# Sums of feed-forward weights formed in scratch by accumulating DMAs, and preparation steps placed after every pair

## Chip, cores, metric

The kernel runs on one core of one Trainium2 chip. The metric is the device time of one execution in microseconds (us); lower is better.

## What is computed

One step of a two-layer decoder trunk over 536 token columns (528 prompt positions and 8 samples), all in float32:

```
x += 0.5 * FFN1(rms(x));  x += MIX(rms(x));  x += 0.5 * FFN2(rms(x))     in each of 2 layers
swiglu(h) = (silu(h @ W_gate) * (h @ W_up)) @ W_down       1024 -> 2 x 2816 -> 1024
MIX of layer 0: convolution module and sliding-window attention; MIX of layer 1: a complex-diagonal state-space model (SSM)
a last RMSNorm follows
```

There are thus four feed-forwards, called FF1 (layer 0, first), FF2 (layer 0, second), FF3 (layer 1, first) and FF4 (layer 1, second) here. The output also holds the convolution, key, value and SSM states.

## The kernel before, in words

**Layout.** The activations stand transposed: `x[0..7]` are eight tiles of 128 model rows by 536 token columns, in two halves of 268. `xh` and `xl` are x times the norm's gain, split into a part that TensorE takes exactly and the rest; `eh`, `el`, `fh`, `fl` hold sums and differences of them. A product of a weight tile (`whi`, `wlo`: 128 x 128) with such a pair takes three matmuls of 268 columns: hi by hi, hi by lo, lo by hi.

**One feed-forward** is `ffn` (L401). The 2816 hidden columns are 22 tiles of 128, in three chunks of 6, 8 and 8 (`CHUNKS`, L33). The first two hidden tiles (three in FF1) are made by `pair` (L383): the gate gemm, then `rstd` (L304), which makes the normaliser `R` out of one matmul, a ScalarE operation and eight VectorE operations (`rsqrt`, L290), then the up gemm, then the evacuation by VectorE with R (L395 to L398) and the split `put` (L145). Between the pairs, `operands(k)` (L187) makes the sums and differences for four k, seven VectorE operations each (with `put`), and `settle` (L206) moves a part of them.

All other hidden tiles, 20 per feed-forward and 19 in FF1, are made by `seven` (L246), called a *pair* (gate and up) here. It forms the four quarter products of the two halves of the tokens with seven products instead of eight (a scheme of Strassen's kind): 7 x 4 x 3 = 84 matmuls (L266). `SLOTS` (L32) gives the order, in which a pair's last two products run among the next pair's first. `seven_weights` (L212) loads gate and up weights G and U (two DMAs of 512 KB, L220, L221), splits G, and forms on VectorE

```
q = U0 + U1        (L228)      0, 1: the upper and lower half of the 1024 model rows
U0 = U0 + G0       (L229)
G0 = G0 + q        (L230)      G1 = G1 + G0 (L234)
```

and splits all of them: the high part by ScalarE (L224), the low part by VectorE (L225). G and U take turns in four `raw` buffers; the split weights of one pair fill the three `whi` and three `wlo` buffers. After a chunk, its down projection runs over eight tiles of model rows (called column tiles here): a gemm (L139, L142) of the chunk's hidden tiles, and an addition to x on VectorE (L434); after the last chunk also `finalize` (L151).

**Preparation.** `setup0` (L440) prepares the layer 0 mixer beside FF1, and `ssm_prep` (L909) the SSM beside FF2 and FF3: parameters by series of small VectorE operations, powers `pw` (L981), powers E of the transition (L999 to L1027, complex products through `cmul`, L895), and for each of eight j the tables B, C, K and T (L1029 to L1086), written to scratch by POOL's DMA queue and read back by the mixer. Both are Python generators: `fill` (L405) draws steps from them, and only the down loops call it (L437): one step per column tile in the first chunk, two in the second, one for the first four of the last, 28 per feed-forward.

**Order of work.** Each engine runs its instructions in one fixed order, which the framework's list scheduler derives when the kernel is built, out of program order and a timeline of its own; an operation that this timeline takes to be ready may be put well ahead of its place in the program. Weight DMAs are issued from SP's queue, preparation's from POOL's (some from ScalarE's).

## Time and profile before

| | |
|---|---|
| median of 3 runs | 2019.54 us (2015.43 to 2019.72) |
| the profiled execution | 2020.43 us |
| its span, first to last instruction | 2018.6 us |
| TensorE busy (PE) | 1933.7 us, 96% |
| VectorE busy (DVE) | 1577.0 us, 78% |
| ScalarE busy (ACT) | 938.1 us, 46% |
| GpSimd busy (POOL) | 81.4 us, 4% |
| mean granted TensorE clock | 0.984 of full |

The engines run beside each other, so shares don't add up. A row of busy time by stretch gives the stretch in us from the span's start, its length, the busy us and in brackets the count of instructions for PE (matmuls), PEld (weight loads), DVE, ACT and POOL, the granted clock of TensorE as a share of full speed, the busy share of the 16 DMA engines, and GB/s. Overlapping instructions of one engine count once in a stretch; the mean in ns of a group by line is that of one instruction with its overlap. A wait row gives the engine and operation that waited, what ended the wait, the sum in us, how often and the longest. In a timeline the brackets at the end give the idle time before the operation and what ended it.

FF1 runs from about 55 to 422 us, FF2 from 656 to 1048, FF3 from 1048 to 1433, FF4 from 1635 to the end.

### The profile page before, as it was taken

What the parts mean: (1) busy time and instruction counts of PE and PEld (TensorE: products, weight loads), DVE (VectorE), ACT (ScalarE), POOL (GpSimd) and SP (SyncE); (2) the same over time, 40 slices, a digit from 0 to 9 for tenths busy, and PEclk for the clock granted to TensorE, in tenths of its full rate; (3) what the DMA queues carried; (4) which work ended last, traced back from release to release, by engine and by line L of the source; (5) the groups of instructions that cost most, each with busy time, mean ns of one, the idle gap of its engine ahead of it and who ended that gap; (6) DMA issues with size and microseconds to landing.
All of it is one profiled execution on the core that took longest, in us unless ns stands there. A gap on an engine that the chain in (4) does not pass through costs nothing.

```text
span 2018.6 us, 37789 instructions
## 1 busy us (share of the span) xinstructions
PE 1933.7 (96%) x15338; PEld 1870.4 (93%) x15338; DVE 1577.0 (78%) x2799; ACT 938.1 (46%) x1639; POOL 81.4 (4%) x160
## 2 busy tenths in 40 slices
PE   6999999999999899999999999999989999999998
PEld 5999999998779899898999999999989999999997
DVE  5768769678868999989789997696694486794876
ACT  5535435434446635435465354354324364452543
POOL 2000000000000000020001210000110000000000
PEclk9899999999989999999999999999999999999999
DMA  6233333321005234353334543236583323333231
GB/s 185 81 107 87 95 95 95 116 75 44 27 22 123 65 94 127 121 156 113 102 94 120 163 130 103 86 102 193 164 261 101 90 63 95 95 111 89 84 105 53
DMA packets 372066, 213.51 MB, mean 106 GB/s; under 512 B 36299, under 2 KB 362503, under 8 KB 371869
## 3 DMA queue, kind: packets, MB, share of 16 engines
q1 hardware_dynamic: 354901, 190.63, 32.8%
q0 software_dynamic: 6432, 19.40, 3.0%
q10 hardware_dynamic: 10560, 1.09, 0.4%
q8 instruction: 120, 1.97, 0.4%
q14 instruction: 53, 0.43, 0.1%
HBM read 193.14 MB, written 23.65 MB: 107 GB/s over the span
## 4 chain that ended last, share of the span: by engine, by line
PE 73%; DVE 14%; DMA 5%; issue 4%; ACT 3%; ACTq 0%; POOL 0%; SPq 0%; DVEq 0%; POOLq 0%
PE mm L266 25%; PE mm L139 18%; PE mm L142 9%; PE S L139 7%; PE S L266 4%; PE S L142 4%; DMA raw<-in_ffn_w_gu 3%; DVE wlo L225 2%; PE S L747 1%; ACT whi L128 1%; DVE ml L149 1%; DVE wlo L129 1%; DVE ql L225 1%; DMA pb<-in_x_prompt 1%; DVE raw L229 1%
## 5 line engine op out<-in xcount | busy, mean ns | idle before, releaser
L224 ACT ACTIVATE whi<-raw 128x1024 fp32r<-128x1024 f32 (+1 forms) x237 | 216.9, 916 | 184.1 <-PE mm L266 50.5
L128 ACT ACTIVATE whi<-raw 128x1024 fp32r<-128x1024 f32 (+2 forms) x166 | 159.6, 973 | 303.3 <-PE mm L139 156.7
L139 PE MATMUL mm<-mh,whi 128*128 128x268 f32 x1224 | 262.1, 291 | 5.9 <-ACT whi L128 3.0
L225 DVE TENSOR_TENSOR wlo<-raw,whi 128x1024 fp32r<-128x1024 f32 (+1 forms) x237 | 246.7, 1041 | 25.5 <-ACT whi L224 24.7
L139 PE MATMUL mm<-ml,whi 128*128 128x268 f32 x1224 | 259.5, 287 | 0.1
L142 PE MATMUL mm<-mh,wlo 128*128 128x268 f32 x1224 | 259.5, 288 | 0.1
L129 DVE TENSOR_TENSOR wlo<-raw,whi 128x1024 fp32r<-128x1024 f32 (+2 forms) x166 | 184.5, 1117 | 70.1 <-ACT whi L128 67.7
L139 PEld LDWEIGHTS mm<-mh,whi 128*128 128x128 f32 x1224 | 194.5, 190 | 10.6 <-ACT whi L128 4.1
L142 PEld LDWEIGHTS mm<-mh,wlo 128*128 128x128 f32 x1224 | 194.5, 189 | 1.6 <-DVE wlo L129 1.2
L139 PEld LDWEIGHTS mm<-ml,whi 128*128 128x128 f32 x1224 | 194.9, 189 | 0.7 <-DVE ml L149 0.4
L266 PE MATMUL mm<-xh,whi 128*128 128x268 f32 x632 | 183.6, 291 | 5.9 <-ACT sn L274 5.3
L266 PE MATMUL mm<-eh,wlo 128*128 128x268 f32 x632 | 181.5, 287 | 3.2 <-DVE wlo L225 3.2
L266 PE MATMUL mm<-eh,whi 128*128 128x268 f32 x632 | 182.4, 289 | 1.8 <-ACT whi L224 1.1
L266 PE MATMUL mm<-xh,wlo 128*128 128x268 f32 x632 | 181.0, 286 | 0.0
L266 PE MATMUL mm<-xl,whi 128*128 128x268 f32 x632 | 180.8, 286 | 0.0
L266 PE MATMUL mm<-el,whi 128*128 128x268 f32 x632 | 180.6, 286 | 0.0
L266 PEld LDWEIGHTS mm<-xh,whi 128*128 128x128 f32 x632 | 119.0, 188 | 10.6 <-ACT sn L274 9.6
L139 PE MATMUL S<-mh,whi 128*128 128x268 f32 x568 | 121.3, 289 | 3.0 <-ACT mh L148 1.6
L266 PEld LDWEIGHTS mm<-eh,wlo 128*128 128x128 f32 x632 | 118.8, 188 | 4.2 <-DVE wlo L225 4.0
L266 PEld LDWEIGHTS mm<-eh,whi 128*128 128x128 f32 x632 | 119.1, 188 | 3.6 <-ACT whi L224 1.6
L142 PE MATMUL S<-mh,wlo 128*128 128x268 f32 x568 | 120.1, 287 | 0.3 <-DVE wlo L129 0.3
L266 PEld LDWEIGHTS mm<-xl,whi 128*128 128x128 f32 x632 | 119.1, 189 | 0.0
(520 smaller groups left out, 5079.7 us busy)
## 6 DMA issues: line engine op xcount, KB each, us to landing
raw<-in_ffn_w_gu SPq DMA_DIRECT2D x174, 512.0 KB
raw<-in_ffn_w_down SPq DMA_DIRECT2D x64, 512.0 KB
raw<-in_ffn_w_down SPq DMA_DIRECT2D x32, 384.0 KB
raw<-in_ssm_w_glu SPq DMA_DIRECT2D x16, 512.0 KB
raw<-in_ab_w_in SPq DMA_DIRECT2D x10, 512.0 KB
dB<-B POOLq DMA_DIRECT2D x16, 256.0 KB, 2.9
dC<-Z POOLq DMA_DIRECT2D x32, 128.0 KB, 3.2
dT<-dK POOLq DMA_DIRECT2D x8, 512.0 KB, 5.0
```

Of the source, the lines that this page charges most:

```text
L128: nc.scalar.activation(hi[:, :K], raw[:, :K], AF.Copy)
L129: nc.vector.tensor_sub(lo[:, :K], raw[:, :K], hi[:, :K].bitcast(F32))
L139: nc.tensor.matmul(ps[:, h, :HT], hi[:, k, :], src[:, h * HT:(h + 1) * HT], start=(k == 0 and i == 0), stop=False)
L142: nc.tensor.matmul(ps[:, h, :HT], lo[:, k, :], xh[k][:, h * HT:(h + 1) * HT], start=False, stop=(k == K - 1))
L149: nc.vector.tensor_sub(lo, src, hi.bitcast(F32))
L224: nc.scalar.activation(h, r, AF.Copy)
L225: nc.vector.tensor_sub(l, r, h.bitcast(F32))
L229: nc.vector.tensor_add(U[:, k0], U[:, k0], G[:, k0])
L266: nc.tensor.matmul(ps, w[:, c + k, :], b[k], start=bool(first and k + i == 0), stop=bool(last and k == 3 and i == 2), skip_group_check=True)
L747: nc.tensor.matmul(S[:, g, :w], qT[t][rw, 128 * b:128 * b + 128], kT[rw, k0:k0 + w], start=False, stop=True)
```

## The change

For FF2, FF3 and FF4 the first two sums (L228, L229) are no longer made by VectorE. One feed-forward ahead (FF2's during FF1, FF3's during FF2, FF4's during FF3), `presum` forms them in DRAM scratch for all 2816 columns: for each of the two arrays of 512 x 2816, eight slices of 64 rows are copied DRAM to DRAM and the other summand is then added by an accumulating DMA, all from POOL's queue, 32 steps in all. The accumulating DMA of a slice is issued after the copy of the next. `seven_weights` then loads q (into one of two buffers now) and U0 from scratch and only U1 from the weights: four DMAs, 1.25 MB, instead of two with 1 MB.

`fill` is now called after each pair as well as after each column tile, for one step of the preparation each time (44 times per feed-forward, 43 in FF1). With `behind`, the step's instructions on an engine are queued behind given ones: after a pair, VectorE's behind the split of its result; after a column tile, VectorE's behind the addition to x, TensorE's behind the gemm and ScalarE's behind the weights' split. In FF1 to FF3 each call also has POOL copy one column of the tile just made (`go`) and queues a step of `presum` behind that copy. `ssm_prep` gets more yields, so its work is cut into 61 steps instead of 52, and two operations on the C table become one. At a feed-forward's start all four `operands` follow the first `pair`, their VectorE work behind R, and the weight work of the first two pairs of `seven` on VectorE is queued behind the end of the first `pair`. The DMA descriptor scratch is cut to 8192 bytes.

```diff
+    def behind(self, *ins):
+        with ExitStack() as scope:
+            for i in ins:
+                scope.enter_context(self.tc.issue_after(i.ins))
+            yield
...
+    def presum(self, wgu, n):
+        out = [self.dr.tile([512, D_FF], F32, name=f"{a}{n}") for a in ("dP", "dQ")]
+        A = lambda i, j: wgu[512 * j:512 * j + 512, D_FF * i:D_FF * i + D_FF]
+        def steps():
+            late = None
+            for o, a, b in ((out[0], A(1, 0), A(1, 1)), (out[1], A(0, 0), A(1, 0))):
+                for r in range(0, 512, 64):
+                    r = slice(r, r + 64)
+                    nc.gpsimd.dma_start(o[r], a[r])
+                    yield
+                    if late:
+                        nc.gpsimd.dma_start(*late[:2], accum_op=OP.add, max_dma_last_dim=5632)
+                        yield
+                    late = o[r], b[r]
+            nc.gpsimd.dma_start(*late, accum_op=OP.add, max_dma_last_dim=5632)
+            yield
...
-    def seven_weights(self, gu, f):
+    def seven_weights(self, gu, f, sums):
-        q = self.fx.tile([128, 4, 128], F32, name="q4")
+        q = self.fx.tile([128, 4, 128], F32, name="q4", bufs=2)
         nc.sync.dma_start(G[:], gu[:, :, f:f + 128])
-        nc.sync.dma_start(U[:], gu[:, :, D_FF + f:D_FF + f + 128])
+        if sums:
+            part = lambda t: t[:].rearrange("(k p) f -> p k f", p=128)[:, :, f:f + 128]
+            nc.sync.dma_start(q[:], part(sums[0]))
+            nc.sync.dma_start(U[:, k0], part(sums[1]))
+            nc.sync.dma_start(U[:, k1], gu[:, k1, D_FF + f:D_FF + f + 128])
+        else:
+            nc.sync.dma_start(U[:], gu[:, :, D_FF + f:D_FF + f + 128])
...
-        nc.vector.tensor_add(q[:], U[:, k0], U[:, k1])
-        nc.vector.tensor_add(U[:, k0], U[:, k0], G[:, k0])
+        if not sums:
+            nc.vector.tensor_add(q[:], U[:, k0], U[:, k1])
+            nc.vector.tensor_add(U[:, k0], U[:, k0], G[:, k0])
...
-                w = self.seven_weights(gu, (f0 + n0 + n) * 128)
+                with self.behind(*([first] if first and n < 2 else [])):
+                    w = self.seven_weights(gu, (f0 + n0 + n) * 128, sums)
...
-                self.put(self.mh[n0 + n][:], self.ml[n0 + n][:], b[:])
+                fill(1, self.ml[n0 + n], self.put(self.mh[n0 + n][:], self.ml[n0 + n][:], b[:]))
...
-        def fill(n):
-            for _ in range(n):
-                next(filler, None)
+        def fill(n, t, *ins):
+            if n:
+                with self.behind(*ins):
+                    next(filler, None)
+            if pre:
+                i = nc.gpsimd.tensor_copy(self.go[:], t[:, :1].bitcast(F32))
+                with self.behind(i):
+                    next(pre, None)
...
-                for f in range(n0):
-                    self.pair(gu, f, head if f == 0 else None)
-                    for k in range(4 * f // n0, 4 * (f + 1) // n0):
+                first = self.pair(gu, 0, head)
+                for k in range(4):
+                    with self.behind(self.on_r):
                         self.operands(k)
+                for f in range(1, n0):
+                    self.pair(gu, f, None)
...
-                fill((1 if nf < 8 else 2) if not last else int(d < 4))
+                fill(1, self.x[d], i, self.on_pe, self.on_act)
...
-                nc.vector.tensor_add(w[0][:, :576], w[0][:, :576], w[1][:, :576])
-                nc.vector.tensor_scalar(CL[:, :, 1], v(w[0]), -1.0, None, op0=OP.mult)
+                nc.vector.tensor_sub(CL[:, :, 1], v(w[1]), v(w[0]))
...
-    nc = bacc.Bacc("TRN2", target_bir_lowering=False, num_devices=1)
+    nc = bacc.Bacc("TRN2", target_bir_lowering=False, num_devices=1, dynamic_dma_scratch_size=8192)
```

`on_r` is the last VectorE operation of R, `on_pe` the last matmul of the latest gemm, `on_act` the ScalarE split of the latest weight tile.

## Rows read from the trace of the kernel before

**Rows 1.** The page, busy time of TensorE, its share of the span and instructions.
```profile
PE 1933.7 (96%) x15338; PEld 1870.4 (93%) x15338; DVE 1577.0 (78%) x2799; ACT 938.1 (46%) x1639; POOL 81.4 (4%) x160
```

**Rows 2.** Busy time by stretch: FF2, FF3, FF4 but its last columns, FF1.
```profile
656.00:1048.00 392.00, 375.55 (x2975) 366.20 (x2975) 350.51 (x754) 188.99 (x315) 20.08 (x38) 0.99 0.38 111
1048.00:1433.00 385.00, 377.72 (x3046) 369.49 (x3045) 313.32 (x488) 185.72 (x307) 28.32 (x53) 1.00 0.42 125
1635.00:1950.00 315.00, 308.49 (x2450) 304.18 (x2449) 245.95 (x374) 156.18 (x259) 0.00 (x0) 1.00 0.32 93
55.00:422.00 367.00, 362.50 (x2865) 358.00 (x2866) 267.47 (x400) 169.45 (x275) 2.43 (x8) 0.99 0.33 94
```

**Rows 3.** Busy time by stretch: pairs of two chunks of FF2, of FF4; FF2's start.
```profile
756.00:843.00 87.00, 82.93 (x653) 80.96 (x652) 85.49 (x194) 48.17 (x80) 1.63 (x3) 1.00 0.37 111
...
901.00:989.00 88.00, 84.05 (x673) 81.80 (x672) 83.96 (x136) 48.68 (x84) 6.93 (x13) 1.00 0.39 116
...
1732.00:1815.00 83.00, 81.59 (x651) 80.58 (x650) 73.19 (x112) 47.96 (x81) 0.00 (x0) 1.00 0.34 99
...
660.00:664.00 4.00, 2.89 (x24) 2.48 (x23) 4.00 (x11) 2.44 (x6) 0.00 (x0) 1.00 0.00 0
664.00:668.00 4.00, 0.60 (x4) 0.33 (x3) 4.00 (x14) 3.27 (x6) 0.00 (x0) 0.69 0.00 0
668.00:672.00 4.00, 3.99 (x18) 4.00 (x19) 4.00 (x11) 3.28 (x8) 0.00 (x0) 0.50 0.04 12
```

**Rows 4.** Waits of TensorE's weight loads in FF2: us in total, times, longest.
```profile
PEld S L139 <- DVE ta L395: 3.6, 1, 3.6
PEld mm L266 <- DVE wlo L225: 3.5, 3, 1.3
```

**Rows 5.** Groups of instructions by line, whole span.
```profile
L228 DVE TENSOR_TENSOR q<-raw 128x512 f32<-128x512 f32 x79 | 54.4, 689 | 45.1 <-DMA raw<-in_ffn_w_gu 44.7
```

**Rows 6.** Timeline of VectorE at the start of FF2: start, us, operation.
```profile
657.90 0.81 DVE L299 TENSOR_TENSOR tb<-ta 128x268 f32<-128x268 f32 x2 [0.74 <-ACT ta L297]
...
667.25 0.71 DVE L395 TENSOR_TENSOR ta<-S,R 128x536 f32<-128x536 f32 x1
667.87 0.70 DVE L397 TENSOR_TENSOR tb<-mm,R 128x536 f32<-128x536 f32 x1
```

**Rows 7.** Groups by line, VectorE, 656 to 1200 us.
```profile
L1061 DVE TENSOR_TENSOR w<-w,w 128x576 f32<-128x576 f32 x8 | 6.0, 750 | 0.0
...
L887 DVE TENSOR_TENSOR we<-E 128x16 f32<-128x16 f32 (+4 forms) x12 | 3.8, 317 | 0.0
...
L887 DVE TENSOR_TENSOR pt<-E 128x16 f32<-128x16 f32 x12 | 2.2, 182 | 0.0
```

**Rows 8.** Waits of TensorE's weight loads in FF4 without its end.
```profile
PEld mm L139 <- ACT eh L148: 2.5, 1, 2.5
```

**Rows 9.** DMA queues (packets, MB, share of 16 engines) and issues (us to landing).
```profile
q0 software_dynamic: 6432, 19.40, 3.0%
...
dT<-dK POOLq DMA_DIRECT2D x8, 512.0 KB, 5.0
```

**Rows 10.** Timelines of SP's queue and of VectorE beside a pair of FF4.
```profile
1749.95 0.37 SPq L221 DMA_DIRECT2D raw<-in_ffn_w_gu  x1
...
1753.96 0.69 DVE L228 TENSOR_TENSOR q<-raw 128x512 f32<-128x512 f32 x1 [1.24 <-DMA raw<-in_ffn_w_gu]
...
1755.51 1.22 DVE L225 TENSOR_TENSOR wlo<-raw,whi 128x1024 fp32r<-128x1024 f32 x1
...
1758.53 0.69 DVE L230 TENSOR_TENSOR raw<-raw,q 128x512 f32<-128x512 f32 x1
```

**Rows 11.** Timelines of POOL and of VectorE in the SSM mixer.
```profile
1442.43 0.19 POOL L1144 COPY us<-us 128x8 f32<-128x8 f32 x1 [6.36 <-DVE us L1143]
...
1464.61 1.12 POOL L1144 COPY us<-us 128x8 f32<-128x8 f32 x1 [1.51 <-DVE us L1143]
...
1464.46 1.21 DVE L129 TENSOR_TENSOR wlo<-raw,whi 128x1024 fp32r<-128x1024 f32 x1
```

More of the change, by code (lines that the diff above doesn't have):

```diff
@@ L1 @@
-from contextlib import ExitStack
+from contextlib import ExitStack, contextmanager
 import numpy as np
@@ L89, in open @@
         self.R = t("R", F32)
+        self.go = self.cst.tile([128, 1], F32, name="go")
         self.sq = t("sq", F32)
@@ L141, in gemm @@
             for h in hs:
-                nc.tensor.matmul(ps[:, h, :HT], lo[:, k, :], xh[k][:, h * HT:(h + 1) * HT],
-                                 start=False, stop=(k == K - 1))
+                self.on_pe = nc.tensor.matmul(ps[:, h, :HT], lo[:, k, :], xh[k][:, h * HT:(h + 1) * HT],
+                                              start=False, stop=(k == K - 1))
     def put(self, hi, lo, src):
@@ L244, in seven_weights, with seven @@
                 "P7": (uh, ul, 0, X(self.eh, r), X(self.el, r))}
-    def seven(self, gu, f0, n0, nf):
+    def seven(self, gu, f0, n0, nf, first, sums, fill):
         nc = self.nc
@@ L310, in rstd @@
             nc.tensor.matmul(ps[h], self.ones[:], self.sq[:, hc[h]], start=True, stop=True)
-        self.rsqrt([self.R[:, c] for c in hc], ps)
+        self.on_r = self.rsqrt([self.R[:, c] for c in hc], ps)
     def load(self, gu):
@@ L416, in ffn @@
                 n0 = 3 if head else 2
-                for f in range(n0):
-                    self.pair(gu, f, head if f == 0 else None)
-                    for k in range(4 * f // n0, 4 * (f + 1) // n0):
+                first = self.pair(gu, 0, head)
+                for k in range(4):
+                    with self.behind(self.on_r):
                         self.operands(k)
+                for f in range(1, n0):
+                    self.pair(gu, f, None)
                 self.settle()
-            self.seven(gu, f0, n0, nf)
+            self.seven(gu, f0, n0, nf, first if f0 == 0 else None, sums, fill)
             dn = wdn[f0 * 128:(f0 + nf) * 128].rearrange("(k p) f -> p k f", p=128)
@@ L981, in ssm_prep @@
         for k in range(8):
+            if k % 2 == 0:
+                yield
             self.cmul(pw[:, 0, :, k + 1], pw[:, 1, :, k + 1], pw[:, 0, :, k], pw[:, 1, :, k],
@@ L1011, in ssm_prep @@
                         bc = lambda a: a[:, :, m:m + 1].to_broadcast([128, 16, n - 1])
-                        self.cmul(e[0][:, :, m + 1:m + n], e[1][:, :, m + 1:m + n], e[0][:, :, 1:n], e[1][:, :, 1:n],
-                                  bc(e[0]), bc(e[1]), w1, w2)
+                        steps = self.cmul_steps(e[0][:, :, m + 1:m + n], e[1][:, :, m + 1:m + n], e[0][:, :, 1:n], e[1][:, :, 1:n],
+                                                bc(e[0]), bc(e[1]), w1, w2)
+                        for _ in steps:
+                            if n > 16:
+                                yield
                         if n > 4:
@@ L1394, in run @@
             prep = self.ssm_prep(p)
-            self.ffn(io["ffn2_w_gu"][0], io["ffn2_w_down"][0], 3, prep)
-            self.ffn(io["ffn1_w_gu"][1], io["ffn1_w_down"][1], 4, prep)
+            more, pre = self.presum(io["ffn1_w_gu"][1], 1)
+            self.ffn(io["ffn2_w_gu"][0], io["ffn2_w_down"][0], 3, prep, sums, pre)
+            self.finish(pre)
+            sums, pre = self.presum(io["ffn2_w_gu"][1], 2)
+            self.ffn(io["ffn1_w_gu"][1], io["ffn1_w_down"][1], 4, prep, more, pre)
             self.finish(prep)
+            self.finish(pre)
         self.mixer1(5)
-        self.ffn(io["ffn2_w_gu"][1], io["ffn2_w_down"][1], None, fin=True)
+        self.ffn(io["ffn2_w_gu"][1], io["ffn2_w_down"][1], None, sums=sums, fin=True)
 def constants():
```

27 lines of the change are left out of this document (18 added, 9 removed).

## The prediction

> **What bounds the kernel now.** I read the page first, then the busy time by feed-forward and by stage, then the waits of the weight loads of TensorE, and last the timelines of VectorE and the queues at the places where TensorE stood still. The page shows TensorE busy for 1933.7 of 2018.6 us [rows 1]. The change takes no matmul away, so time can be won only from the 85 us in which TensorE idles. FF1 to FF4 are the four feed-forwards in the order in which they run. TensorE idles for 392 - 375.55 = 16.5 us in FF2, 385 - 377.72 = 7.3 in FF3, 315 - 308.49 = 6.5 in the part of FF4 shown and 367 - 362.50 = 4.5 in FF1 [rows 2]. FF1 has the same loops and almost no preparation beside them; its 4.5 us are my floor for what stays. A matmul takes 308.49 / 2450 = 0.126 us [rows 2].
>
> Why FF2 is worse: VectorE is busy for 85.5 of 87 us and 84.0 of 88 us beside the eight pairs of its second and third chunk, and for 73.2 of 83 us beside the same eight pairs in FF4, where nothing is prepared [rows 3]. So the preparation of the SSM fills VectorE, and TensorE waits for weight splits and for evacuations by VectorE: 3.5 us and 3.6 us are the longest two rows of FF2's waits [rows 4].
>
> **The change, part by part.**
>
> *The two additions.* Each pair of FF2 to FF4 loses the adds of L228 and L229, 0.689 us busy for the one [rows 5] and, being of the same shape, as much for the other. Neighbours on VectorE start a little before the one ahead has ended (two of 0.71 us start 0.62 apart [rows 6]), so I count 0.60 each: 1.2 us for each of 20 pairs, 24 us per feed-forward. Only the part that lies where VectorE is the bound counts. A pair takes TensorE 83 / 8 = 10.4 us; VectorE needs 73.2 / 8 = 9.15 us of it now and 7.95 after, which leaves 2.4 us beside a pair for a preparation step.
>
> *The preparation steps* were pulled 28 times per feed-forward, all in the down loops (two per column tile in the second chunk), and are now pulled once after each of 20 pairs and 24 column tiles, 44 times. There are 61 of them instead of 52, so 44 run in FF2 and 17 in FF3. I count which step falls where from the yields. The first chunk takes the small ones. The eight pairs of the second chunk take eight of the ten steps of the powers E. These cost six lines like L887's 12 x 0.317 and six like its 12 x 0.182 us [rows 7], 6 x 3.8 + 6 x 2.2 = 36 us with overlaps, some 27 without, 20 of it on those eight pairs: 2.5 to 3 us per pair. With 7.95 that is 10.5 to 11, no less than TensorE's 10.4. I expect nothing from these pairs; their 87 - 82.9 = 4.1 us idle stays. The third chunk's steps belong to the tiles j: five steps for six operations of the size of L228, six of the size of L1061 (0.75 us [rows 7]) and some small ones; a scaling besides is dropped. That is 6 x 0.69 + 6 x 0.75 + 0.6 = 9.2 us, under 1.8 per step with the overlaps taken off, 9.7 with the pair, below 10.4. Of the 88 - 84.05 = 3.95 us idle there [rows 3] I take 2.5, since FF4's pairs keep 83 - 81.59 = 1.4. From FF2's other stretches, the down loops above all, I take 1.5.
>
> *The start of a feed-forward.* In FF2 the normaliser R begins at 657.90, and the first evacuation that needs it starts at 667.25 [rows 6], because operand and weight work is mixed in between the eight operations of R. TensorE idles for 1.1 and 3.4 us from 660 to 668, and its granted clock is 0.69 of full, then 0.50 (the lower level, 1.2 GHz): 18 matmuls in 4 us where 0.126 us each would give 32, 1.8 us more [rows 3]. In all 6.3 us. The change puts the operands behind R, the first two pairs' weight work behind pair 0, and the preparation later; eight operations of some 0.4 us [rows 6] then end near 661.5 and TensorE hardly stops. It gives some back: about two of four operand groups, seven operations each (six of 268 columns, of which two took 0.81 us [rows 6], and one of 536 at 0.62: 3 us), ran ahead of R and now follow it, 6 us later for the sixth product of the first pair, against 2.4 us of adds gone. I take +4 in FF2, between 0 and 6.3. In FF3 and FF4 the same order is a gain of at most the 2.5 us that FF4 waits there [rows 8] and a loss of at most 3 each; I take 0 and +1. From the rest of FF3 (7.3 less the floor of 4.5, half of it) I take 1.5.
>
> *The sums in scratch.* Each of FF1, FF2, FF3 gets 16 copies and 16 accumulating transfers of 64 x 2816 x 4 B = 0.72 MB, paced by one step per pair or column tile. The POOL queue's packets took 3.0% of 16 engines for 19.40 MB, 3.1 us per MB [rows 9]: a copy is 2.25 us of all engines. No accumulating transfer is in the trace. Its ends are 2.25 us (a copy) and 21 us (three passes, each at the 5.0 us that dT's DRAM-to-DRAM 0.52 MB needs to land [rows 9], scaled up to 7 us). I take 4.5, twice a copy, because it reads twice as much and the queue's own rate is the nearest row. What it can hurt are weight loads. In FF4 the up half was issued at 1749.95, VectorE's add waited for it until 1753.96, and the result is first needed at 1758.53 [rows 10]: 3.9 us to spare after the add's 0.69. In FF1, which still adds, 2.25 us is covered by that and 4.5 is not quite; I take a loss of 1.5 us (0 to 15). In FF2 to FF4 the first sum is loaded by itself into one of two buffers, ahead of the up half, and two sums are no longer in the chain, so the cover grows; the 256 KB more per pair and two more issues (0.37 us each on SP's queue [rows 10]) I cost at nothing behind it.
>
> *POOL.* After each pair and column tile of FF1 to FF3 POOL copies one column to pace itself, 43 + 44 + 44 = 131 copies, with the transfers and the preparation's own queued behind them. POOL is busy for 20 and 28 us of FF2 and FF3 [rows 2], so it has the time. A copy of 128x8 took 0.19 us at 1442.43 and 1.12 us at 1464.61, where it ended together with a VectorE operation of 1.21 us that had begun before it [rows 11]; elsewhere an operation of that shape takes 1.22 us [rows 10]. So POOL waits and VectorE does not: nothing. The Trainium skill, SBUF — State Buffer, section "Who interferes with whom", says that whichever of the two starts first holds their shared port for its whole instruction, so the copy could as well hold VectorE up. By that rule the sum would lose up to 1.12 us per copy; the rows show the other order.
>
> *The sum.* FF2 2.5 + 1.5 + 4 = 8; FF3 1.5; FF4 1; FF1 -1.5: 9 us. The profiled execution took 2020.43 us, 1.8 more than its span and 0.9 more than the median, 2019.54. 2020.4 - 9 = 2011.4, and less 0.9 that is **2010.5 us**.
>
> **The rivals.**
> *VectorE stays the bound (0.22).* The relief of 24 us in FF2 is eaten: as much preparation is now pulled in FF2 (44 of 61 steps against 28 of 52), the E steps fall on pairs, and the operands behind R delay three starts. For it: 10.5 to 11 against 10.4 us; against it: the third chunk has room. It keeps 2.5 + 1.5 of the gains and loses 1.5: 2017.
> *The accumulating transfers hold up the weights; slower (0.18).* If one occupies the engines for 9 us, each of the eight that lie beside pairs of FF1 delays a load by up to 9 - 3.9 = 5.1 us, half of them or half of that seen by TensorE: 8 x 2.6 = 20 us against 9 won, 2030. It decides from about 5.2 us per transfer, where 8 x 1.3 eats the gain. For it: DMA engines are already busy 38 and 42% of FF2 and FF3 [rows 2]. Against it: they are far from full.
> *POOL's copies hold VectorE (0.04).* 44 x 1.12 = 49 us more in FF2 would leave VectorE at 350.5 - 24 + 49 of 392, the bound again, and about 12 us worse in all: 2032. This is the skill's rule with the other order of starts.
> My forecast has 0.56.
>
> **How the numbers follow.** A measurement of this kernel can tell about 0.2%, 4 us, from no change. The forecast's case is faster nearly throughout (0.54 of 0.56). The second splits 0.08 faster, 0.12 same, 0.02 slower. The third and fourth are slower but for 0.01. Together 0.62 faster, 0.15 same, 0.23 slower. The range starts where all idle time above the floor goes (FF2 12 + 1.8, FF3 2.8, FF4 2.5, about 19 us, 2000, less 1) and reaches to the third case, 2030; the forecast's own range is 2001 to 2016.
>
> **What would show it.** Right: L228 and L229 only 19 times; the idle of TensorE in FF2 down to about 8 us; R's first evacuation within 5 us of R's start and no fall of the clock there; FF1 within 2 us of its 367. Wrong: in FF1 longer waits of VectorE for weight loads than before, with TensorE waiting for splits; or VectorE full beside FF2's second-chunk pairs with TensorE as idle as before; or a new stall at the sixth product at the start of FF3 and FF4.

## The result and the profile after

The changed kernel took **2073.15 us** (median of 4 runs, 2070.96 to 2076.23), the kernel before beside it 2019.63: a ratio of **1.027 (1.0246 to 1.0291)**, 54 us slower. The forecast was 2010.5, in a range of 1999 to 2030. Both the sign and the range were wrong.

The profile page of the changed kernel, its rows of busy time, of two DMA queues (packets, MB, share of 16 engines) and of the transfers (KB each, median us from issue to landing), to be read against [rows 1, 9]:

```profile
PE 1955.0 (94%) x15338; PEld 1888.9 (91%) x15338; DVE 1506.4 (73%) x2671; ACT 934.5 (45%) x1639; POOL 248.1 (12%) x387
...
q1 hardware_dynamic: 387541, 206.37, 34.4%
q0 software_dynamic: 17184, 88.61, 16.8%
...
dP<-in_ffn_w_gu POOLq DMA_DIRECT2D x48, 704.0 KB, 7.0
dQ<-in_ffn_w_gu POOLq DMA_DIRECT2D x48, 704.0 KB, 6.8
```

VectorE lost 1577.0 - 1506.4 = 70.6 us of work, as the change meant. The time got longer all the same. Busy time by stretch, FF1, FF2, FF3 and FF4 of the changed kernel (columns as in [rows 2]):

```profile
core 0: us, PE busy (x) PEld busy (x) DVE busy (x) ACT busy (x) POOL busy (x), PEclk, DMA share, GB/s
53.00:449.00 396.00, 370.20 (x2846) 360.54 (x2845) 269.34 (x417) 172.02 (x283) 53.73 (x85) 0.98 0.54 146
677.00:1092.00 415.00, 386.35 (x3027) 376.58 (x3027) 338.90 (x741) 189.04 (x319) 89.08 (x127) 0.98 0.65 178
1092.00:1488.00 396.00, 378.22 (x3009) 371.15 (x3008) 288.41 (x442) 186.79 (x309) 75.36 (x116) 0.98 0.68 186
1689.00:2004.00 315.00, 309.70 (x2456) 306.69 (x2455) 228.99 (x349) 157.47 (x266) 0.00 (x0) 0.99 0.37 107
```

TensorE now idles for 25.8 us in FF1 (4.5 before), 28.7 in FF2 (16.5) and 17.8 in FF3 (7.3) [rows 2]. These three are the feed-forwards with transfers beside them. FF4, without any, idles for 5.3 (6.5; a part of what its start loses is busy time at a lower clock, below). FF1 is the plainest: it uses no sums, has next to no preparation, and is 29 us longer. Its groups by line show where that comes from. First the addition of the kernel before in the window of FF1, then the same one after:

```profile
L228 DVE TENSOR_TENSOR q<-raw 128x512 f32<-128x512 f32 x18 | 12.4, 690 | 10.1 <-DMA raw<-in_ffn_w_gu 9.9
```

```profile
L267 DVE TENSOR_TENSOR q<-raw 128x512 f32<-128x512 f32 x19 | 13.1, 689 | 39.5 <-DMA raw<-in_ffn_w_gu 39.5
```

VectorE stood still for 39.5 us ahead of this addition, waiting for a weight load; before it was 9.9. TensorE meets that a little later, as waits for evacuations and splits. The waits of TensorE's weight loads in FF1, two of the kernel before and then the four longest of the changed kernel (us in total, times, longest; L314 and L317 of the changed kernel are L274 and L277 of the one before, and no wait of `seven` for a split, L224 or L225, is among its rows):

```profile
PEld mm L266 <- ACT sn L274: 2.7, 6, 0.7
...
PEld mm L266 <- DVE tb L277: 0.4, 1, 0.4
```

```profile
PEld mm L306 <- ACT sn L314: 7.5, 7, 1.7
PEld mm L306 <- DVE tb L317: 6.3, 7, 1.2
PEld mm L306 <- ACT whi L262: 6.1, 3, 3.5
PEld mm L306 <- DVE wlo L263: 5.0, 2, 4.6
```

### The profile page after: what moved, and what is told of

Its sections match the earlier page's. It is cut to its first block, busy times and chain, and to the rows that moved or that the text cites. A ratio compares the mean times of both kernels' runs of the same rounds, so it can differ in the third digit from the quotient of the medians.

```text
span 2073.8 us, 38318 instructions
## 1 busy us (share of the span) xinstructions
PE 1955.0 (94%) x15338; PEld 1888.9 (91%) x15338; DVE 1506.4 (73%) x2671; ACT 934.5 (45%) x1639; POOL 248.1 (12%) x387
## 3 DMA queue, kind: packets, MB, share of 16 engines
q0 software_dynamic: 17184, 88.61, 16.8%
## 4 chain that ended last, share of the span: by engine, by line
PE 72%; DVE 9%; DMA 8%; ACT 3%; issue 2%; ACTq 0%; SPq 0%; DVEq 0%; POOLq 0%
PE mm L306 29%; PE mm L148 15%; PE mm L151 8%; PE S L148 6%; DMA raw<-in_ffn_w_gu 5%; PE S L306 5%; PE S L151 3%; DVE wlo L263 2%; DMA raw<-in_ffn_w_down 1%; PE S L796 1%; ACT whi L262 1%; DMA dE<-E 1%; ACT whi L129 1%; DVE ml L158 1%; DVE wlo L130 1%
## 5 line engine op out<-in xcount | busy, mean ns | idle before, releaser
L306 PE MATMUL mm<-xh,whi 128*128 128x268 f32 x632 | 186.7, 296 | 20.6 <-ACT whi L262 8.4
L306 PE MATMUL mm<-xh,wlo 128*128 128x268 f32 x632 | 185.8, 294 | 3.5 <-DVE wlo L263 3.5
L306 PEld LDWEIGHTS mm<-eh,whi 128*128 128x128 f32 x632 | 121.7, 193 | 17.8 <-ACT sn L310 15.9
L306 PEld LDWEIGHTS mm<-xh,wlo 128*128 128x128 f32 x632 | 122.5, 194 | 4.4 <-DVE wlo L263 4.2
## 6 DMA issues: line engine op xcount, KB each, us to landing
raw<-in_ffn_w_down SPq DMA_DIRECT2D x32, 384.0 KB
```

What stands on the lines that cost most here:

```text
L306: nc.tensor.matmul(ps, w[:, c + k, :], b[k], start=bool(first and k + i == 0), stop=bool(last and k == 3 and i == 2), skip_group_check=True)
```

## The experiments

Ratios are to the kernel before on the same chip, with a 95% interval. "Stage" times are differences between the ends of VectorE's evacuations in the traces of one execution each; the time of a feed-forward runs from the first VectorE operation of its R to the addition of its last column tile (FF4: to the end). One thing about the code first: in `seven` the parameter `first` is overwritten by the start flag of the first product, so the changed kernel holds only the first pair's weights behind pair 0, not those of two.

### Which part costs: transfers and start undone

The theory to begin with was that the transfers starve the weight loads, above all beside column tiles; the rival, that the new start and the order of the steps cost.

**Transfers out.** `presum` issues nothing, and the loads of the sums read plain weights. POOL's pacing copies stay.

```
-        return out, steps()
+        return [A(1, 0), A(0, 0)], iter(())
```

> The changed kernel without any transfer into scratch: the loads that read sums read weights of the same shape instead, so q and U0 hold plain weights and the output of the feed-forwards is not the reference's; POOL's pacing copies stay. Theory 1 (the transfers' packets of 5.6 and 11.3 KB starve the weight queue's packets of 512 B, above all in the down loops): the 8 to 9 us that each first-chunk down loop of FF1 to FF3 has lost come back, FF1 is as long as before, and the whole is about 45 us faster than the changed kernel, 2025 to 2032. Theory 2 (the new order of the start and of the preparation is what costs): at most 10 us faster than the changed kernel, 2063 or more.

**Old start.** The operands spread between the first pairs as before, nothing held behind R or pair 0.

```
-                for k in range(4):
-                    with self.behind(self.on_r):
-                        self.operands(k)
+                    for k in range(4 * f // n0, 4 * (f + 1) // n0):
+                        self.operands(k)
```

> The changed kernel with the operands spread between the first pairs as before and nothing queued behind R or pair 0. Theory 1: the start costs little beside the transfers; from R to the last pair of the first chunk FF2, FF3 and FF4 had become 2, 3.5 and 6.5 us longer, so at most 12 us come back, 2061 to 2067. Theory 2: 30 us or more come back, below 2045.

**Both.**

> Both undone: no transfer (weights read in place of the sums, so again not the reference's output), and the operands at a start as before. What is left is the gain that the change was to bring: two adds less per pair and the preparation beside every pair. Theory 1 and my forecast of that part: 8 to 13 us faster than before, 2007 to 2013. Theory 2 (preparation beside pairs fills VectorE): no faster than before, 2018 to 2035.

**Transfers alone.** The kernel before with the 96 transfers and the pacing copies beside it, their results unused.

```
+                pace(self.ml[n0 + n])       # beside every pair
+                pace(self.x[d])             # beside every column tile
```

> The kernel before with the 96 transfers, POOL's pacing copies and the smaller descriptor scratch of the change beside it, at the same places; the results are read by nobody, all adds and the old order stay. Theory 1: FF1, FF2 and FF3 grow by some 15 us each, 2060 to 2075, and nothing else changes. Theory 2: within 8 us of before, below 2028.

| | new start | old start |
|---|---|---|
| with transfers | 2073.15, 1.0268 (1.0246 to 1.0291) | 2052.54, 1.017 (1.0149 to 1.0191) |
| without | 2031.32, 1.0057 (1.004 to 1.0075) | 2011.89, 0.997 (0.9953 to 0.9987) |

The transfers cost 41.8 us with the new start and 40.6 with the old one; the new start costs 20.6 and 19.4. The two hardly touch each other. The run without transfers came out as the theory said; the old start alone fell between the two cases, since both causes are there. What is left with both undone gains 0.3%. In the kernel before, whose VectorE has more to do, the transfers alone made it 2109.85 us, 1.0453 (1.0417 to 1.0489): twice their cost in the changed kernel, and more than either case expected.

### Where the transfers cost

With the transfers and without (old start in both), FF1 takes 396.7 for 374.2 us, FF2 389.8 for 374.7 and FF3 381.1 for 375.5. Stage times put the largest part into the column tiles after the first chunk, where the loop of eight should take 30 us:

| stage | without | with |
|---|---|---|
| first chunk's column tiles, FF1 / FF2 / FF3 | 30.5 / 31.9 / 30.4 | 37.8 / 39.1 / 39.3 |
| FF1: second chunk from first to last pair, its column tiles | 77.4, 36.8 | 82.6, 40.4 |
| FF1: third chunk's first pair, the other seven | 20.5, 77.6 | 25.5, 81.9 |
| second chunk's first pair, FF1 / FF2 / FF3 | 23.1 / 20.1 / 27.2 | 20.0 / 21.1 / 23.1 |
| FF2: second chunk from first to last pair, its column tiles, third chunk's first pair | 76.2, 39.3, 22.3 | 77.3, 43.2, 24.8 |
| FF3: second and third chunk's pairs | 74.1, 75.1 | 74.1, 75.1 |

That is 23.4 us in the first row, of which the pair behind gives 6 back, 18 in the rest of FF1, 7 beside the second chunk of FF2, and nothing beside the later pairs of FF3. POOL's timeline at this place in FF1 of the changed kernel:

```profile
118.34 1.06 POOL L236 DMA_DIRECT2D dP<-in_ffn_w_gu  x1 [0.36 <-issue]
...
122.22 0.55 POOL L233 DMA_DIRECT2D dP<-in_ffn_w_gu  x1 [0.28 <-issue]
...
123.09 0.97 POOL L236 DMA_DIRECT2D dP<-in_ffn_w_gu  x1
...
124.79 0.53 POOL L233 DMA_DIRECT2D dP<-in_ffn_w_gu  x1
...
129.03 0.96 POOL L236 DMA_DIRECT2D dP<-in_ffn_w_gu  x1
...
133.13 0.53 POOL L233 DMA_DIRECT2D dP<-in_ffn_w_gu  x1 [0.26 <-issue]
```

Six transfers in 15 us. One takes 3.0 us of all 16 engines: the queue's share rose from 3.0% [rows 9] of 2018.6 us to 16.8% of 2073.8, 288 us more for 96. The packet records of the changed kernel's trace tell the two kinds apart: 3,072 packets of 11,264 bytes make 2.0 us for a copy, 6,144 of 5,632 bytes 4.0 us for an accumulate. Six are 18 us of engine time in 15, beside the weight loads. The chain of waits shows the load that suffered, with its addition behind it:

```profile
125.70 18.09 DMA raw<-in_ffn_w_gu
143.79 0.02 issue
143.82 0.70 DVE q L267
```

A load that took about 4 us beside a pair of FF4 [rows 10] held the chain for 18.1; its issue alone held SP's queue for 11.2 us, where that of [rows 10] took 0.37. **None in the first chunk** tests that: old start, big packets, no transfer beside the first chunk, what is left over two at a time in the third. (Not to a column tile alone, as the expectation has it: `ins` is not empty behind pairs either, and the trace has two transfers behind each pair of FF1's third chunk.)

```
-            if pre:
+            if pre and f0:
                 ...
+                    if last and ins:
+                        next(pre, None)
```

> The changed kernel with the old start (2052.5 us), its 96 transfers in their big packets, but none beside a feed-forward's first chunk; the ones left over go two to a column tile in the third chunk. The first chunk's down loops took 37.8, 39.1 and 39.3 us with transfers and 30.5, 31.9 and 30.4 without, 23 of the 41 us that the transfers cost. If it is the burst of transfers in that stage that costs (they are more than the engines can move in the time): about 2030, up to 2038 us with what the third chunk's pairs of transfers cost. If a transfer costs the same wherever it stands: 2048 to 2056 us.

2034.51 us, 1.0063 (1.0048 to 1.0078): 18 of the 41 us are gone. The first chunk's column tiles are back at 30.7, 31.8 and 30.7 us. That agrees with the 23.4 less 6 of the table. So it is shown that the transfers issued in this stage cost what is lost there. FF1 gains next to nothing in all (394.8 for 396.7 us), since the doubled transfers take it back in its third chunk (87.3 us for 77.6 without transfers).

### Packets or bytes

In the changed kernel the transfers' packets are 11,264 and 5,632 bytes, those of a weight load 512. The Trainium skill (DMA: Bandwidth & Descriptors, "Queues, rings and completion order") says that an engine alternates between its queues and drains a whole packet of one before it turns to the next; a packet there holds several descriptors, so it need not be what the profile counts as one. The trace agrees as far as the queues' shares go: by the packet records the weight queue had 0.10 to 0.15 of the engines from 128 to 137 us of the changed kernel, while big packets ran beside it, and 0.33 to 0.50 from 129 to 150 us of the first run below, with small ones. My theory 1a was that a load beside a queue of big packets gets few bytes, and that equal packets would give it half of the engine.

```
-                    nc.gpsimd.dma_start(o[r], a[r])
+                    nc.gpsimd.dma_start(o[r], a[r], max_dma_last_dim=512)      # and 5632 -> 512 for both accumulates
```

> The changed kernel with the same 96 transfers cut into packets of 512 bytes, the size of a weight load's, in place of 11,264 (copies) and 5,632 (accumulates). Theory 1a (what starves the weight loads is the size of the packets: an engine that serves its queues packet by packet spends 490 ns on a transfer's and 28 ns on a weight load's, so the load keeps a few per cent of the engine): with equal packets the loads keep half of the engine, most of the 41 us that the transfers cost comes back, 2031 to 2050 us. Theory 1b (the engines' time for the bytes is what lacks, whatever the packets): 2065 to 2080 us. If the small packets make the accumulates dearer, each a read and a write of its own, it is slower than the changed kernel, over 2080 us.

> The small packets, and the operands of a feed-forward spread between its first pairs as in the kernel before, nothing held behind the norm or the first pair. The start gave 19 to 21 us in both settings measured, so this is the small-packet run less 20 us: theory 1a 2011 to 2030 us, theory 1b 2045 to 2060 us.

> The run without transfers in the first chunk (2034.5 us, big packets), with the small packets. Without transfers at all it is 2011.9. What is left of their cost stands beside the first feed-forward's second and third chunk: 3.5 us in the second chunk's pairs, 4.2 in its down loop, 5.5 and 9.7 in the third chunk's pairs. If there the packets starve the weight loads and not the bytes: 2016 to 2024 us. If the bytes: 2031 to 2038 us.

2066.69 us, 1.023 (1.0212 to 1.0249), with the new start; 2040.9, 1.0111 (1.0087 to 1.0135), with the old one; and without the first chunk's transfers 2050.74, 1.0149 (1.0127 to 1.0171), **16 us slower** than with big packets. The first fits the rival (bytes), the second lies between the two cases, the third is slower than both. Rows of the page of the first of them, to be held against those of the changed kernel above:

```profile
q0 software_dynamic: 84000, 88.61, 21.2%
...
dP<-in_ffn_w_gu POOLq DMA_DIRECT2D x48, 704.0 KB, 9.6
```

The packet counts say that the accumulates came out at 512 bytes and the copies at 4,096 (48 x 1408 + 48 x 176 packets are the 84,000 less the 7,968 that both kernels have besides). The same bytes now take (0.212 x 2069.3 - 60.6) / 96 = 3.9 us of all engines for 3.0; by the packet records a copy still takes 2.0 us, an accumulate 5.9 for 4.0. The stages, with the old start, show that the small packets free the loads in some places and cost time in others:

| stage | none | big | small |
|---|---|---|---|
| first chunk's column tiles, FF1 / FF2 / FF3 | 30.5 / 31.9 / 30.4 | 37.8 / 39.1 / 39.3 | 37.6 / 32.9 / 34.6 |
| FF1: second chunk's pairs, third chunk's first pair, the other seven | 77.4, 20.5, 77.6 | 82.6, 25.5, 81.9 | 77.0, 21.5, 78.0 |
| FF2: second chunk's pairs, its column tiles | 76.2, 39.3 | 77.3, 43.2 | 80.7, 46.3 |

In FF1's later chunks, and beside the first chunk of FF2 and FF3, most of the loss comes back (half of it in FF3), though the engines have more to do (busy for 1.03 and 1.06 of these two stretches, for 0.83 and 0.84 with big packets; packet times overlap, so that a share can pass 1). There the size of the packets makes most of the loss, and not the engines' time. FF2's second chunk gets longer, and all of the 16 us of the third run are in FF2 (397.5 for 381.3 us); that this is the dearer accumulate was not tried apart. Beside FF1's first chunk small packets change nothing. The engines are busy there for 0.84 of the stretch with big packets and 1.04 with small ones, against 0.37 in the kernel before. The rows are the changed kernel, the small packets and the kernel before (new start in the first two):

```profile
116.00:154.00 38.00, 34.41 (x260) 33.61 (x259) 19.07 (x33) 9.66 (x14) 8.86 (x16) 0.93 0.84 219
```

```profile
120.00:159.00 39.00, 34.56 (x263) 34.20 (x262) 19.59 (x34) 9.66 (x14) 12.75 (x17) 0.93 1.04 204
```

```profile
118.00:147.00 29.00, 28.96 (x233) 28.56 (x232) 17.51 (x25) 8.13 (x11) 0.00 (x0) 1.00 0.37 104
```

Why FF1's first chunk gained nothing, though the weight queue's share rose there, stays open, and so does how the 41 us divide between packet size and bytes: smaller packets change both.

### The start

**Operands late, weights free.** Without transfers, the operands behind the norm, the first pair's weights not held.

```
-            self.seven(gu, f0, n0, nf, first if f0 == 0 else None, sums, fill)
+            self.seven(gu, f0, n0, nf, None, sums, fill)
```

> The changed kernel without its transfers (the sums' loads read plain weights in their place), its operands still behind the norm, but the weights of the first seven-product pair no longer held behind the first plain pair. With both rules it took 2031.3 us, with neither 2011.9. If the operands behind the norm are what costs: 2028 to 2033 us; if the weights that are held: 2010 to 2014; if both share it: about 2022.

2033.67 us, 1.0069 (1.0048 to 1.0091): as much as with both rules (2031.32). The operands behind R are the whole 20 us; holding the weights costs nothing that can be seen. From R to the split of the last pair of the first chunk this run took 76.1, 83.0 and 76.2 us in FF2 to FF4, for 70.9, 74.4 and 70.5 with the old start: 5.2 + 8.6 + 5.7 = 19.5. (FF2's second chunk took another 7 us from first to last pair, 83.2 for 76.2, and 4 came back ahead of FF3; for neither is a cause shown.) The start of FF4 in the changed kernel, by stretch:

```profile
core 0: us, PE busy (x) PEld busy (x) DVE busy (x) ACT busy (x) POOL busy (x), PEclk, DMA share, GB/s
1686.00:1707.00 21.00, 21.00 (x169) 20.86 (x168) 16.38 (x34) 15.54 (x27) 0.00 (x0) 1.00 0.19 53
1707.00:1712.00 5.00, 2.52 (x19) 2.09 (x17) 5.00 (x10) 4.57 (x8) 0.00 (x0) 1.00 0.39 114
1712.00:1719.00 7.00, 5.64 (x25) 5.64 (x26) 6.51 (x14) 3.97 (x10) 0.00 (x0) 0.51 0.25 74
1719.00:1730.00 11.00, 10.56 (x83) 10.12 (x82) 5.16 (x9) 4.74 (x8) 0.00 (x0) 1.00 0.25 73
```

And four lines of VectorE's timeline there: the split in front of R, the first operand, a weight split, and the last operand work.

```profile
1688.92 1.23 DVE L130 TENSOR_TENSOR wlo<-raw,whi 128x1024 fp32r<-128x1024 f32 x1 [3.54 <-ACT whi L129]
...
1693.25 0.43 DVE L203 TENSOR_TENSOR u<-ou 128x268 f32<-128x268 f32 x1
...
1712.09 1.22 DVE L263 TENSOR_TENSOR wlo<-raw,whi 128x1024 fp32r<-128x1024 f32 x1
...
1718.69 0.44 DVE L158 TENSOR_TENSOR fl<-u,fh 128x268 fp32r<-128x268 f32 x1 [0.49 <-ACT fh L157]
```

The same place in the kernel before: the end of the norm's sums, an operand, the split in front of R, and the end of R.

```profile
1631.81 0.71 DVE L165 TENSOR_TENSOR sq<-sq,ta 128x536 f32<-128x536 f32 x1
...
1634.81 0.44 DVE L194 TENSOR_TENSOR u<-ou 128x268 f32<-128x268 f32 x1
...
1635.99 1.22 DVE L129 TENSOR_TENSOR wlo<-raw,whi 128x1024 fp32r<-128x1024 f32 x1
...
1643.47 0.78 DVE L302 TENSOR_TENSOR R<-ta,tb 128x268 f32<-128x268 f32 x2
```

R is indeed short, as hoped: it is done at 1693. But VectorE idled for 3.5 us just ahead of the split in front of it, while the operands that used to stand there waited; afterwards all 28 operand operations compete with the splits of the first pairs. From 1707 VectorE is full, TensorE gets 2.5 us of work in 5, and then its clock stands at 0.51, the lower level of 1.2 GHz, for the next 7 us.

### Steps, sums and the second buffer

**Steps alone**: old start, no transfers, all additions kept; of the change only the steps beside every pair remain.

```
-            self.ffn(io["ffn2_w_gu"][0], io["ffn2_w_down"][0], 3, prep, sums, pre)
+            self.ffn(io["ffn2_w_gu"][0], io["ffn2_w_down"][0], 3, prep)
```

> The old start, no transfers, all four feed-forwards add on VectorE as before; of the change only the preparation steps beside every pair and their finer cut are left. If the relief of 8.7 us is that of the sums no longer made on VectorE: 2017 to 2023 us, as before. If the steps' placement gives it: 2010 to 2014 us.

**Sums left out alone**: the kernel before with two of four additions of FF2 to FF4 dropped and plain weights read in their place, as in the first experiment.

```
-        nc.vector.tensor_add(q[:], U[:, k0], U[:, k1])
-        nc.vector.tensor_add(U[:, k0], U[:, k0], G[:, k0])
+        if not sums:
+            nc.vector.tensor_add(q[:], U[:, k0], U[:, k1])
+            nc.vector.tensor_add(U[:, k0], U[:, k0], G[:, k0])
```

> The kernel before, its order of the preparation steps and its start kept, with two of the four weight sums of the second to fourth feed-forward left out: the loads read plain weights in their place, and no transfer makes the sums. With steps beside every pair the sums' leaving gave 22.4 us (2034.3 to 2011.9), and those steps alone cost 13.1 (2021.1 to 2034.3). If the two are independent: 1996 to 2001 us. If they are the same VectorE time counted twice (the steps cost because the sums are there): 2006 to 2013 us, which is what the prediction's relief would make it.

The steps came out at 2034.27 us, 1.0068 (1.0053 to 1.0083), slower than both cases expected. The sums alone gave 2013.48, 0.9962 (0.995 to 0.9974), half a us outside the case "counted twice". What I had not seen is that both kernels, and all others so far but the transfers alone, hold one more thing of the change: a second buffer for `q`, and the smaller DMA scratch that makes room for it.

```
-        q = self.fx.tile([128, 4, 128], F32, name="q4")
+        q = self.fx.tile([128, 4, 128], F32, name="q4", bufs=2)
-    nc = bacc.Bacc("TRN2", ..., num_devices=1)
+    nc = bacc.Bacc("TRN2", ..., num_devices=1, dynamic_dma_scratch_size=8192)
```

**Buffer and scratch alone**, then **the scratch alone**, each in the kernel before:

> The kernel before with nothing of the change but the second buffer of the tile for the upper sum and the smaller DMA scratch that makes room for it. All four kernels built from the kernel before with these two reach the end of the first pairs 3.5 to 5.5 us later than it, and in one of them VectorE waits 8 us there for a load, with the upper sum's addition queued ahead of a pair's evacuation. If the second buffer does it (the sum's addition is put ahead of work that is due earlier): 2 to 6 us slower than before, 2022 to 2026 us. If not: 2019 to 2021.

> The kernel before with the smaller DMA scratch alone, and one buffer for the upper sum: its instructions stand in the same order as before on every engine. If the 19 us of the run with both come from the second buffer (which puts additions ahead of other work in VectorE's and TensorE's order): within 2 us of before, 2018 to 2024 us. If the scratch (room for fewer descriptors of the software queue) does it: about 2040 us.

With both 2040.48 us, 1.0097 (1.0078 to 1.0117); with the scratch alone 2018.91, 1.0004 (0.9989 to 1.0019), its instructions in the old order on every engine. So the second buffer costs **19.6 us**, where I expected 2 to 6. It changes no operation and lets the list scheduler put the addition further ahead. VectorE's timeline in FF1's start, in the kernel with the second buffer:

```profile
54.98 0.43 DVE L302 TENSOR_TENSOR R<-ta,tb 128x268 f32<-128x268 f32 x1
59.66 0.69 DVE L228 TENSOR_TENSOR q<-raw 128x512 f32<-128x512 f32 x1 [4.26 <-DMA raw<-in_ffn_w_gu]
60.27 0.43 DVE L302 TENSOR_TENSOR R<-ta,tb 128x268 f32<-128x268 f32 x1
...
61.92 0.70 DVE L395 TENSOR_TENSOR ta<-mm,R 128x536 f32<-128x536 f32 x1
```

and in the kernel before:

```profile
53.46 0.78 DVE L302 TENSOR_TENSOR R<-ta,tb 128x268 f32<-128x268 f32 x2
54.16 0.43 DVE L149 TENSOR_TENSOR fl<-u,fh 128x268 fp32r<-128x268 f32 x1
54.50 0.70 DVE L395 TENSOR_TENSOR ta<-mm,R 128x536 f32<-128x536 f32 x1
```

With one buffer, the second pair's `q` must wait until the first's has been split, so it cannot stand here. With two, it stands between the two halves of R; its load lands 4.3 us too late, and R's second half and the first evacuation wait behind it, until 61.92 for 54.50. In the profiled executions FF1 has lost 6 us up to the next norm, FF2 loses another 7; the rest is spread over the SSM mixer (6), FF4 (4) and FF3 (2). The rows show the mechanism at FF1's start alone, and for the mixer's share I have none.

Five of these runs, each one step further than the one above it, make up the whole:

| kernel | ratio | step, of 2020 us |
|---|---|---|
| before + second buffer | 1.0097 | +19.6 |
| + steps beside every pair | 1.0068 | -5.9 |
| + sums left out | 0.997 | -19.8 |
| + operands behind the norm | 1.0057 | +17.6 |
| + transfers: the changed kernel | 1.0268 | +42.6 |

Each step is uncertain by about 5 us, and the table holds in its order alone (POOL's pacing copies come in with its third row). Without the additions the second buffer has less to harm: from the buffer alone to the sums left out as well, with the old steps, is -27 us (1.0097 to 0.9962), and the steps then add +1.6. What the sums are worth with one buffer in all three feed-forwards, and what the second buffer costs in the changed kernel, was not run.

### Is there a place where the transfers pay?

**FF2's sums in the mixer**: old start, steps beside every pair, FF2's 32 transfers issued in the mixer ahead of it, the others not made. **Sums where there seemed room**: the kernel before, FF2's as just said, FF4's beside the later chunks of FF3. **FF2's alone**, and **with one of FF4's** in the same mixer. **FF2's, one buffer**: the third of these with one `q` buffer and the full scratch. In the mixer each step of it lets POOL issue one transfer:

```
+            i = nc.gpsimd.tensor_copy(self.go[:], t[:, :1].bitcast(F32))
+            with self.behind(i):
+                next(self.pre, None)
```

> The old start, and sums in scratch for the second feed-forward alone, their 32 transfers issued through the mixer between the first and second feed-forward, where the DMA engines are busy 6 to 28% of the time; the third and fourth feed-forward add on VectorE as before. Theory 1 (the transfers cost only where weight loads need the engines): the transfers cost 0 to 4 us, and the second feed-forward keeps its relief: 2009 to 2018 us. Rival (the relief of 8.7 us is that of the preparation steps beside every pair, and not of the sums that are no longer made on VectorE): the same as the steps alone within 2 us.

> The kernel before, its order and start kept, with the sums made in scratch only where the runs show room: those of the second feed-forward during the mixer in front of it, those of the fourth beside the second and third chunk of the third (where transfers moved no time of a stage), the third adding on VectorE as before. Theory: the second feed-forward gains about 4 to 6 us less 2 to 3 for the transfers in the mixer, the fourth about 5 to 8 us, so 2008 to 2015 us. Rival: the transfers take back what the sums give here too, 2018 to 2030 us.

> The kernel before, its order of steps and its start kept, with the sums of the second feed-forward alone made in scratch, in the mixer in front of it. In the run with sums where there seemed room, the second feed-forward took 388.1 us from norm to norm (393.5 before), and the mixer no longer than without transfers (231.7 and 232.4 us). If that holds alone: 5 us faster than before, 2013 to 2017 us. If the gain there is one profile's luck: within 2 us of before.

> The same, and the first of the two sums of the fourth feed-forward made in the same mixer (48 transfers there in place of 32). The fourth feed-forward gained 6 us from norm to last pair with both sums left out, so half of them should give 2 to 4 us: 2010 to 2014 us, if the mixer still hides the transfers; if 48 are too many for it (48 by some 3 us of all engines is 144 of its 190 us, beside a share of 0.13 of its own), 2016 to 2026 us.

> The sums of the second feed-forward alone, made in the mixer (2029.5 us), with one buffer for the upper sum and the full scratch as in the kernel before. If the second buffer cost 4 to 9 us there: 2013 to 2024 us, and only at its lower end a gain over the kernel before. If it cost nothing: 2027 to 2032 us.

The first four missed: 2024.21 (1.0015, 1.0003 to 1.0027), 2042.88 (1.012, 1.0104 to 1.0136), 2029.5 (1.0045, 1.0032 to 1.0059) and 2031.88 (1.0061, 1.0045 to 1.0077). All four have the second buffer. Against the steps alone (1.0068) the first gains 11 us, so the rival, that only the steps bring relief, is out too. With half of FF4's sums in the mixer too, FF4 took 8 us less (376.1 for 384.0 in the run with FF2's alone), and the stretch with the mixer, from FF1's last column tile to FF2's R, 8 more (249.3 for 241.5). The second also shows where FF4's transfers hurt when FF3 still adds: in the chain of waits, a weight load of the SSM mixer, and the stretch at the end of FF3:

```profile
1414.36 20.87 DMA raw<-in_ssm_w_in
```

```profile
1406.00:1443.00 37.00, 36.83 (x294) 36.23 (x293) 22.95 (x30) 17.23 (x24) 10.05 (x17) 1.00 1.07 314
```

The mixer's loads and tables meet the last transfers, and the engines are full (1.07). Without the second buffer, FF2's sums take 2017.2 us against 2021.64, **0.9983 (0.9968 to 0.9997)**: 12 us better than the same with two buffers, and the only version with correct sums that comes out below both kernels. As one of eighteen runs, with an interval that ends just under 1, it shows a gain that is likely and no more.

## Why the prediction was wrong

- **The additions** went: 19 of them are left (the row of L267), and VectorE is busy for 70.6 us less. Their gain and that of the steps were put at 2.5 + 1.5 in FF2 and 1.5 in FF3, 5.5 us. With the transfers and the start undone the kernel gains 0.3%, 6 us. This agreement is luck: by feed-forward, in one profile each, it comes from FF2 (374.7 for 384.4 us, with 4 us lost again ahead of FF3) and from FF4 (374.9 for 380.9), where I had put nothing for the additions; FF3 stays (375.5 for 375.4), and FF1 is longer (374.2 for 369.1), as it is with the second buffer alone (373.8). Beside FF2's second-chunk pairs I expected nothing, and they take 76.2 us for 82.9. By the table the sums' leaving gives 20, the steps 6, and the second buffer takes 20 back, in that order of steps alone.
- **"into one of two buffers ... so the cover grows"** is a step that failed. I read the second buffer as more cover for a load. What it does to the order of instructions I did not ask, though the order is derived from what each operation has to wait for; it costs 19.6 us in the kernel before. A loss of 5 us in FF1, as there, is found again without transfers and with the old start; the rest was not measured in the changed kernel. The wait of VectorE for loads [rows 5] was the row that should have made me ask: an in-order engine pays for an operation that stands too early.
- **"The start of a feed-forward", a gain of 4 us in FF2, 0 in FF3 and 1 in FF4**, is the second that failed, by sign: losses of 5.2, 8.6 and 5.7 without transfers. I saw that the operands would be late for the sixth product of the first pair, took 2.3 us off the 6.3 for it in FF2, and netted it to nothing in FF3. The idle 3.5 us ahead of R in FF4 was what the old order used for them, and a stall there is followed by a stretch at the lower clock, which I had counted as a gain of 1.8 us in [rows 3] and not as a loss.
- **"The sums in scratch", a loss of 1.5 us**, is the largest: 41. The duration was right: a copy and an accumulate were taken at 2.25 and 4.5 us of all engines, and 2.0 and 4.0 were measured. What failed is where they stand and how many come at once. 3.9 us to spare is the cover beside a pair; I priced a single transfer against it, in FF1 alone, and charged nothing beside column tiles, where the pace is one for every 3.7 us instead of one for every 10 and several come at once, and nothing in FF2 and FF3, which lost 15 and 6 us beside FF1's 22.5. The 0 to 15 that I gave as its bounds came from the same sum. That a load has to share the engines with much bigger packets was not in the sum either.
- **The rival "accumulating transfers hold up the weights"** had the right mechanism, and its sign in FF1 (VectorE waiting for loads, TensorE for splits) is what the rows show. I made its price, 20 us, hang on a transfer of 9 us, and it decided from 5.2, "each of the eight that lie beside pairs of FF1" by itself. It decided at 4.0, with several at once.
- **POOL's copies**: nothing, as said, as far as runs tell. With them and without the transfers it took 2011.89 us; without either, 2013.48. They differ in the steps too. VectorE's addition took 689 ns in the mean in FF1 of the changed kernel, for 690 before: nothing of a wait for POOL is to be seen there.
- **The rival "VectorE stays the bound"** did not come about: VectorE is busy for 338.9 of 415 us in FF2. Without transfers and with the old start it is still busy for 72.9 of 76.2 us beside the second chunk's pairs, but TensorE idles there for only 0.2.

## What to carry to other kernels

Price background transfers by the rate at which their pacing lets them go, stage by stage, against the engine time left in the densest stage; a mean share of 40% says nothing about six transfers in 15 us. Look at their packets beside those of the loads as well: smaller ones freed the loads in some stages here and lost time in others. A buffer more is a change of order wherever a scheduler places operations as soon as they could run: compare the order of the instructions with one buffer and with two before counting it as cover. And before moving work behind an operation in order to shorten that one, look at what the engine did in the wait ahead of it.

## What was not expected of the hardware

- An accumulating transfer of 704 KB, from the weights into scratch, takes 4.0 us of all 16 engines, twice a copy of the same bytes (2.0), by the packet records of the changed kernel; in 512-byte packets it takes 5.9. A limit of 512 bytes left the copies' packets at 4,096.
- One weight load of 512 KB beside these transfers took 18.1 us with its issue, one beside the end of FF3 20.9.
- The transfers cost twice as much, 89 us, beside the kernel before than beside the changed one, with the same bytes. There all additions wait for loads. That this is why was not tried.
